# Moving eight subtractions to GpSimd and four weight combinations ahead of the scalings in an MLP up pass

## The chip, the core and the metric

The kernel runs on one core of a Trainium2 chip. Each core has TensorE (PE, matrix products), VectorE (DVE), ScalarE (ACT), GpSimd (POOL) and SyncE (SP, which here issues the transfers). The metric is the device time of one execution in microseconds. Before the change it is 2866.62 us, the median of three runs (2863.16 to 2868.66).

## The reference

The program is a two-layer backbone over 1024 latent tokens and 256 context tokens with model width 1024. Each layer runs token mixers under one input projection, an output projection, and then a squared-ReLU MLP of inner width 4096:

```python
def sq_relu_mlp(h, w1, w2):
    return jnp.square(jax.nn.relu(h @ w1)) @ w2

x = x + g1 * (y @ w_out[l])
h = rmsnorm(x, norm2_g[l]) * (1.0 + sc2) + sh2
x = x + g2 * sq_relu_mlp(h, w_mlp1[l], w_mlp2[l])
```

The context tokens go through the same steps in layer 0 only. The change is in the product `h @ w1` for the latent tokens, the up pass, and in the preparation of its operands.

## The kernel before

**Float32 products from rounded parts.** TensorE multiplies a rounded format. Each operand `a` is therefore split in two: a high part `hi`, which ScalarE makes by a cast, and a low part `lo = a - hi`, a subtraction on VectorE. One product of two split operands takes three matmuls (hi·hi, hi·lo, lo·hi; function `mm3`, lines 94 to 96). The helper `parts` (L1097 to L1100) makes one split: the cast is L1098, the subtraction L1099. In the profile both appear under these lines for nearly every operand of the kernel, so one goes by the names of the tiles.

**Seven products instead of eight.** The up pass multiplies a 2 x 2 arrangement of blocks by a scheme in the manner of Strassen and Winograd. The input `h` (transposed, width by tokens) is cut into width halves and token halves: `11` and `21` (first 512 tokens, group 1) and the second 512 tokens, group 2, which yield `22`. Out of these come the combined operands `T1`, `T2`, `T3`, `T4`. Every operand is four tiles of 128 x 512. On the weights' side, a block `j` of 256 output columns gives two chunks `r[0]`, `r[1]` (128 x 1024 each) and from them two combined chunks: `sa` (L1185, L1186) and `sb` (L1191, L1192). Product numbers and operands: 1 with `11`, 2 with `21`, 5 with `T1`, 7 with `T3`, 6 with `T2`, 3 with `22`, 4 with `T4`. Each product is 4 x 3 = 12 matmuls of 128 x 512.

**The stage around the change.** When the output projection has finished group 1, its tokens are normalized, scaled and split, so operands `11` and `21` are ready early. Group 2 comes last. Meanwhile `prep(j, 0)` splits the first weight chunk of blocks 0 to 3 (the "lead"), and TensorE works at `lead()`: products 1 and 2 of these four blocks. During that time `combine` (L1110 to L1154) scales group 2 (`scaled`: L1106 on VectorE, L1107 on ScalarE), forms the combinations, and splits them: first T1 (L1135), then T3 (L1140), then T2 (L1144) together with the high part of `22` (the cast L1147) and the difference for T4 (L1145); then the four low parts of `22` (L1150); and at the end T4's splits. The low parts of T2, T3 and T4 lie in a shared set of tiles named `x`, those of T1 and `22` in tiles named `al`. In between come `prep(0, 1)` (load both chunks of block 0, form `sa`, split it), `prep(0, 2)` (form `sb`, split it) and `prep(0, 3)` (split the second chunk).

**After it.** `rest` goes through the products 5, 7, 6, 3, 4 of each block. Product 7 is written to a fresh PSUM bank, VectorE adds that bank onto a tile (`v`, L1263), and product 4 is later accumulated into the same bank, so it may begin only when L1263 has read it. L1268 does the same for product 6, without a later use of its bank. For later blocks, `prep(j + 1, i)` runs between the products.

**What sets the order.** Apart from the opening stage, the order on each engine is laid out by the framework's planner before the run: it takes instructions by program order and by when its own cost model thinks them ready. On the chip each engine, and SP's queue of transfers, then works its list strictly in that order and waits at an instruction whose input isn't there. The weight chunks go through two buffers `wraw`; a load waits until the previous user of its buffer has been read.

**GpSimd before.** It runs some subtractions of the same kind in `load_y` (L1058), a few products and memsets, and nothing in the stage of this change.

Of the kernel before, what the change touches and what calls it, by code (L numbers as in the profile page):

```python
# [11 lines left out]
F32 = mybir.dt.float32  # L12
# [25 lines left out]
def fview(a):  # L38
    return a.bitcast(F32)
# [8 lines left out]
class Kern:  # L48
# [1045 lines left out]

    def parts(self, src, hi, lo):  # L1097
        ins = self.nc.scalar.copy(hi, src)  # L1098
        self.nc.vector.tensor_sub(lo, src, fview(hi))  # L1099
        return ins  # L1100

    def scaled(self, x, r, gi, A, sh, f):
# [7 lines left out]
    def combine(self, x, A, sh, hi, lo, tp_, xp, out):  # L1110


        nc = self.nc
        h1 = [xf(x, 1, k) for k in range(KT)]
        h2 = [xf(x, 2, k) for k in range(KT)]
        H = KT // 2
        th = {n: [tp_.tile([128, 512], F32R, name=f"th{n}", bufs=H) for _ in range(H)] for n in (2, 3, 4)}
        tl = {n: [] for n in th}

        def low(n):  # L1120

            tl[n].append(xp.tile([128, 512], F32R, name="x", bufs=XB))
            return tl[n][-1][:]

        def halves(gi):
            return [[a[gi] for a in z[i:i + H]] for i in (0, H) for z in (hi, lo)]

        b11h, b11l, b21h, b21l = halves(1)
        t1h, t1l, b22h, b22l = halves(2)
        out.update({"11": (b11h, b11l), "21": (b21h, b21l), "T1": (t1h, t1l), "22": (b22h, b22l)})  # L1130
        out.update({f"T{n}": (th[n], tl[n]) for n in th})
        r = yield
        for k in range(H):
            self.scaled(x, r, 2, A, sh, k)
            nc.vector.tensor_sub(h1[k], h2[k], h1[k])  # L1135
            self.parts(h1[k], t1h[k][:], t1l[k][:])
            yield
        for k in range(H):
            self.scaled(x, r, 2, A, sh, k + H)
            nc.vector.tensor_sub(h2[k], h2[k + H], h2[k])  # L1140
            self.parts(h2[k], th[3][k][:], low(3))
            yield
        for k in range(H):
            nc.vector.tensor_sub(h1[k], h2[k + H], h1[k])  # L1144
            nc.vector.tensor_sub(h1[k + H], h1[k + H], h1[k])  # L1145
            self.parts(h1[k], th[2][k][:], low(2))
            nc.scalar.copy(b22h[k][:], h2[k + H])  # L1147
            yield
        for k in range(H):
            nc.vector.tensor_sub(b22l[k][:], h2[k + H], fview(b22h[k][:]))  # L1150
        yield
        for k in range(H):
            self.parts(h1[k + H], th[4][k][:], low(4))
            yield  # L1154

    def up(self, l, ctx, B, hi, lo, hp_, hid, filler, last):


        nc, d = self.nc, self.d
        NP, LEAD = DFF // 256, 4  # L1160
        W, E = {}, {}

        def chunk(j, m):
            raw = self.wp.tile([128, 1024], F32, name="wraw", bufs=WRAW)
            nc.sync.dma_start(raw[:], d["w1"][l, 2 * j + m])
            return raw

        def split(src, o=0):
            h, g = (self.wp.tile([128, 1024], F32R, name=n, bufs=WB) for n in ("whi", "wlo"))
            self.parts(src[:, o:], h[:, o:], g[:, o:])  # L1170
            return h, g

        def prep(j, i):

            if i == 0:
                W[j] = [chunk(j, 0)], {}
                W[j][1][0] = split(W[j][0][0])
                return
            r, t = W[j]
            if i == 1:  # L1180
                if j < LEAD:
                    r[:] = [chunk(j, 0)]
                r.append(chunk(j, 1))
                s = hp_.tile([128, 1024], F32, name="sa")
                nc.vector.tensor_add(s[:, :512], r[1][:, :512], r[1][:, 512:])  # L1185
                nc.vector.tensor_sub(s[:, 512:], s[:, :512], r[0][:, :512])  # L1186
                E[j, "sa"] = s
                t[1] = split(s)
            elif i == 2:
                s = hp_.tile([128, 1024], F32, name="sb")  # L1190
                nc.vector.tensor_sub(s[:, :512], r[0][:, :512], r[1][:, :512])  # L1191
                nc.vector.tensor_sub(s[:, 512:], r[0][:, 512:], E[j, "sa"][:, 512:])  # L1192
                t[2] = split(s)
            else:
                t[3] = split(r[1], 0 if ctx else 512)

# [515 lines left out]
    def run(self):  # L1712
        nc, d = self.nc, self.d
        PS = bass.MemoryType.PSUM
        with self.open(name="pad", side="right") as pad, self.open(name="const") as self.cp, self.open(name="w") as self.wp, \
# [13 lines left out]
            hi, lo = self.alloc_act()  # L1729
            with self.open(name="x0") as xp, self.open(name="sp0") as self.sp, self.open(name="ada0") as ap0, self.tc.manual_schedule():  # L1730
                W, accs, Wv = self.opening(xp, ap0, xsrc, hi, lo)
            self.ntmp = 3
            for l in range(DEPTH):
                need_ctx = l < DEPTH - 1
                groups = (0, 1, 2) if need_ctx else (1, 2)
                yh, yl, W, xt = self.mixers(l, xsrc, hi, lo, need_ctx, W, accs, Wv if l == 0 else [])
# [3 lines left out]
                hi, lo = self.alloc_act()  # L1740
# [15 lines left out]
                with self.open(name=f"x{l + 1}", side="right") as xp, self.open(name=f"up{l}") as hp_, contextlib.ExitStack() as right:  # L1756

                    x = {1: [None] * KT, 2: [None] * KT}
                    for gi, f0 in ((2, 0), (1, 0), (2, 4), (1, 4)):
                        for f in range(f0, f0 + 4):  # L1760
                            x[gi][f] = xp.tile([128, 512], F32, name="x", bufs=XB)
                    sh, B = mod[:, 24:32, :], {}
                    prep, lead, rest = self.up(l, need_ctx, B, hi, lo, hp_, hid, ada, start)
                    self.ntmp = 2
                    with self.open(name=f"sp{l + 1}") as self.sp:
                        with self.open(name=f"xc{l + 1}", side="right") as xq:
                            if need_ctx:
                                x.update(self.alloc_x(xq, (0,)))
                            run_all(self.outproj(l, x, xsrc, groups[:-1], yh, yl, W, xt))
                            sums = {gi: self.ssq(x, gi) for gi in groups[:-1]}  # L1770
                            out2 = self.outproj(l, x, xsrc, groups[-1:], yh, yl)
                            for _ in range(3):
                                next(out2)
                            for gi, q in sums.items():
                                keep(x, gi)
                                r = self.rstd(*q)
                                if gi == 0:
                                    self.modulate(x, r, gi, A[1], sh, hi, lo)
                                    next(out2)
                                    continue  # L1780
                                for f in range(KT):
                                    self.parts(self.scaled(x, r, gi, A[1], sh, f), hi[f][gi][:], lo[f][gi][:])
                        self.wide = 1
                        acc = self.sp.tile([128, 512], F32, name="ssq", bufs=2)
                        done = 4 if need_ctx else 3
                        for f in range(done):
                            self.ssq_step(acc, x, 2, f, 0, 512)
                        for f in range(done, KT):
                            next(out2)
                            self.ssq_step(acc, x, 2, f, 0, 512)  # L1790
                            if f >= 4:
                                prep(f - 4, 0)
                        self.wide = 0
                        tp_ = right.enter_context(self.open(name=f"tt{l}", side="right"))
                        blocks = self.combine(x, A[1], sh, hi, lo, tp_, xp, B)
                        next(blocks)
                        next(lead)
                        r = self.rstd(acc, 512)
                        keep(x, 2)
                        next(lead)  # L1800
                        blocks.send(r)
                        for _ in range(3):
                            next(lead)
                            next(blocks)
                        prep(0, 1)
                        next(lead)
                        next(blocks)
                        next(blocks)
                        prep(0, 2)
                        next(lead)  # L1810
                        next(blocks)
                        next(blocks)
                        next(lead)
                        next(blocks)
                        prep(0, 3)
                        run_all(blocks)
                    with self.open(name=f"us{l}") as up_:
                        rest(up_)
                with self.open(name=f"xd{l}") as xp, self.open(name=f"sd{l}") as self.sp, self.open(name=f"we{l}") as wx:
# [35 lines left out]
                    hi, lo = nact  # L1855
# [3 lines left out]
def run_all(g):  # L1859
    for _ in g:  # L1860
        pass
# [148 lines left out]
```

## Time and profile before

| | us |
|---|---|
| Median of the runs | 2866.62 |
| Profiled execution | 2864.0 |
| its span | 2862.2 |
| TensorE busy | 2812.3 |
| VectorE busy | 2206.3 |
| ScalarE busy | 1267.9 |
| GpSimd busy | 105.4 |

The span runs from the first to the last instruction of the profiled execution; the execution's own time is 1.8 us longer. A busy share is an average over stages with different limits, so a stage is judged by its own waits. Matmuls are pipelined: a matmul's row may show 0.39 us while the next one starts 0.23 us behind it. A row of a timeline gives the start, the duration, the engine, the line, the operation, the tiles and, in square brackets, the idle time ahead of it and what ended it. A row of waits reads: who waited, for whom, microseconds in total, times, longest.

### The profile page before, as it was taken

What the parts mean: (1) busy time and instruction counts of PE and PEld (TensorE: products, weight loads), DVE (VectorE), ACT (ScalarE), POOL (GpSimd) and SP (SyncE); (2) the same over time, 40 slices, a digit from 0 to 9 for tenths busy, and PEclk for the clock granted to TensorE, in tenths of its full rate; (3) what the DMA queues carried; (4) which work ended last, traced back from release to release, by engine and by line L of the source; (5) the groups of instructions that cost most, each with busy time, mean ns of one, the idle gap of its engine ahead of it and who ended that gap; (6) DMA issues with size and microseconds to landing.
All of it is one profiled execution on the core that took longest, in us unless ns stands there. A gap on an engine that the chain in (4) does not pass through costs nothing. (4 is left out here: it accounts for less than half of the span.)

```text
span 2862.2 us, 45475 instructions
## 1 busy us (share of the span) xinstructions
PE 2812.3 (98%) x16500; PEld 2376.9 (83%) x16500; DVE 2206.3 (77%) x4917; ACT 1267.9 (44%) x2472; POOL 105.4 (4%) x183
## 2 busy tenths in 40 slices
PE   7999999999999999999999999999999999999998
PEld 4877788889888888888889988888887788888888
DVE  6779988776798777589878768878776887759774
ACT  5333335564553333344545333336555533334443
POOL 1110000010000000000000101000010000000000
PEclk9999999999999999999999999999999999999999
DMA  7433433246446555798977222223346354479672
GB/s 257 145 107 126 144 97 104 91 121 203 152 158 234 189 197 199 262 324 290 327 257 263 72 76 88 71 72 120 119 134 205 129 184 154 145 264 312 211 249 99
DMA packets 279264, 497.40 MB, mean 174 GB/s; under 512 B 23648, under 2 KB 119904, under 8 KB 279040
## 3 DMA queue, kind: packets, MB, share of 16 engines
q1 hardware_dynamic: 279040, 494.50, 51.8%
q8 instruction: 130, 2.13, 0.3%
q14 instruction: 94, 0.77, 0.1%
HBM read 398.82 MB, written 95.59 MB: 173 GB/s over the span
## 5 line engine op out<-in xcount | busy, mean ns | idle before, releaser
L94 PE MATMUL q<-ah,whi 128*128 128x512 f32 (+1 forms) x1472 | 549.9, 374 | 3.3 <-ACT ah L1098 2.7
L96 PE MATMUL q<-ah,wlo 128*128 128x512 f32 (+1 forms) x1472 | 547.4, 372 | 0.8 <-DVE wlo L1099 0.7
L95 PE MATMUL q<-al,whi 128*128 128x512 f32 (+1 forms) x1472 | 548.1, 372 | 0.0
L94 PE MATMUL mm<-ah,whi 128*128 128x512 f32 (+1 forms) x1120 | 387.6, 346 | 2.3 <-ACT whi L88 2.1
L96 PE MATMUL mm<-ah,wlo 128*128 128x512 f32 (+1 forms) x1120 | 385.4, 344 | 0.5 <-DVE wlo L89 0.5
L95 PE MATMUL mm<-al,whi 128*128 128x512 f32 (+1 forms) x1120 | 385.3, 344 | 0.0
L94 PEld LDWEIGHTS q<-ah,whi 128*128 128x128 f32 x1472 | 277.8, 189 | 53.2 <-ACT ah L1098 3.4
L96 PEld LDWEIGHTS q<-ah,wlo 128*128 128x128 f32 x1472 | 277.5, 189 | 50.4 <-DVE wlo L1099 1.7
L95 PEld LDWEIGHTS q<-al,whi 128*128 128x128 f32 x1472 | 277.7, 189 | 48.8 <-issue 1.4
L94 PE MATMUL mm<-whi,ah 128*128 128x512 f32 (+2 forms) x864 | 314.6, 364 | 0.4 <-DVE st L320 0.4
L95 PE MATMUL mm<-wlo,ah 128*128 128x512 f32 (+2 forms) x864 | 307.7, 356 | 0.6 <-DVE wlo L89 0.4
L96 PE MATMUL mm<-whi,al 128*128 128x512 f32 (+2 forms) x864 | 307.5, 356 | 0.0
L94 PEld LDWEIGHTS mm<-ah,whi 128*128 128x128 f32 x1120 | 212.5, 190 | 30.4 <-ACT whi L88 2.5
L96 PEld LDWEIGHTS mm<-ah,wlo 128*128 128x128 f32 x1120 | 212.4, 190 | 26.0 <-DVE wlo L89 1.0
L95 PEld LDWEIGHTS mm<-al,whi 128*128 128x128 f32 x1120 | 212.4, 190 | 25.1 <-issue 0.2
L1098 ACT CAST ah<-raw 128x512 fp32r<-128x512 f32 (+1 forms) x264 | 142.8, 566 | 120.4 <-PE q L96 53.5
L94 PEld LDWEIGHTS mm<-whi,ah 128*128 128x128 f32 x864 | 163.7, 189 | 27.7 <-issue 2.5
L96 PEld LDWEIGHTS mm<-whi,al 128*128 128x128 f32 x864 | 163.7, 189 | 23.2
L95 PEld LDWEIGHTS mm<-wlo,ah 128*128 128x128 f32 x864 | 163.9, 190 | 22.0 <-DVE wlo L89 1.4
L1099 DVE TENSOR_TENSOR al<-raw,ah 128x512 fp32r<-128x512 f32 (+1 forms) x264 | 157.6, 621 | 22.6 <-ACT ah L1098 22.3
L1099 DVE TENSOR_TENSOR wlo<-raw,whi 128x1024 fp32r<-128x1024 f32 x84 | 102.5, 1222 | 74.4 <-ACT whi L1098 71.7
L94 PE MATMUL q<-th,whi 128*128 128x512 f32 x384 | 150.4, 392 | 2.1 <-DVE s L1263 2.0
(306 smaller groups left out, 5232.9 us busy)
## 6 DMA issues: line engine op xcount, KB each, us to landing
raw<-w SPq DMA_DIRECT2D x168, 512.0 KB
raw<-hid SPq DMA_DIRECT2D x104, 512.0 KB
wada<-w_adaT SPq DMA_DIRECT2D x96, 512.0 KB
wraw<-w SPq DMA_DIRECT2D x80, 512.0 KB
hid<-hb SPq DMA_DIRECT2D x128, 256.0 KB
hid<-ht SPq DMA_DIRECT2D x96, 256.0 KB
w<-gscr SPq DMA_DIRECT2D x36, 512.0 KB
wada<-w_ada SPq DMA_DIRECT2D x32, 512.0 KB
```

Of the source, the lines that this page charges most:

```text
L94: mm(out, lh, rh, start=start, stop=False, skip_group_check=True)
L95: mm(out, lh, rl, start=False, stop=False, skip_group_check=True)
L96: mm(out, ll, rh, start=False, stop=stop, skip_group_check=True)
L1098: ins = self.nc.scalar.copy(hi, src)
L1099: self.nc.vector.tensor_sub(lo, src, fview(hi))
```

## The change

`parts` takes an engine for its subtraction. In `combine`, the four low parts of `22` and the four of T4 are made on GpSimd instead of VectorE; those of `22` are now made directly behind their casts, and the loop of its own that they had is gone. In `up`, the four operations that form `sa` and `sb` become functions `mix` and `less`; a new step `prep(0, 4)` calls both for block 0 ahead of `combine`, and with them the loads of block 0's two chunks. `prep(0, 1)` and `prep(0, 2)` then only split. For the other blocks the steps stay as they were.

```diff
-    def parts(self, src, hi, lo):
+    def parts(self, src, hi, lo, eng=None):
         ins = self.nc.scalar.copy(hi, src)
-        self.nc.vector.tensor_sub(lo, src, fview(hi))
+        (eng or self.nc.vector).tensor_sub(lo, src, fview(hi))
         return ins
...
             self.parts(h1[k], th[2][k][:], low(2))
-            nc.scalar.copy(b22h[k][:], h2[k + H])
+            self.parts(h2[k + H], b22h[k][:], b22l[k][:], nc.gpsimd)
             yield
-        for k in range(H):
-            nc.vector.tensor_sub(b22l[k][:], h2[k + H], fview(b22h[k][:]))
         yield
         for k in range(H):
-            self.parts(h1[k + H], th[4][k][:], low(4))
+            self.parts(h1[k + H], th[4][k][:], low(4), nc.gpsimd)
             yield
...
+        def mix(j):
+
+            r = W[j][0]
+            if j < LEAD:
+                r[:] = [chunk(j, 0)]
+            r.append(chunk(j, 1))
+            s = E[j, "sa"] = hp_.tile([128, 1024], F32, name="sa")
+            nc.vector.tensor_add(s[:, :512], r[1][:, :512], r[1][:, 512:])
+            nc.vector.tensor_sub(s[:, 512:], s[:, :512], r[0][:, :512])
+
+        def less(j):
+
+            r = W[j][0]
+            s = E[j, "sb"] = hp_.tile([128, 1024], F32, name="sb")
+            nc.vector.tensor_sub(s[:, :512], r[0][:, :512], r[1][:, :512])
+            nc.vector.tensor_sub(s[:, 512:], r[0][:, 512:], E[j, "sa"][:, 512:])
+            return s
...
+            if i == 4:
+                mix(j)
+                less(j)
+                return
...
             if i == 1:
...
+                if (j, "sa") not in E:
+                    mix(j)
+                t[1] = split(E[j, "sa"])
             elif i == 2:
...
+                t[2] = split(E[j, "sb"] if (j, "sb") in E else less(j))
...
                             if f >= 4:
                                 prep(f - 4, 0)
+                        prep(0, 4)
                         self.wide = 0
                         tp_ = right.enter_context(self.open(name=f"tt{l}", side="right"))
                         blocks = self.combine(x, A[1], sh, hi, lo, tp_, xp, B)
```

More of the change, by code (lines that the diff above doesn't have):

```diff
@@ L1180, in prep @@
             if i == 1:
[L1181 to L1188, printed above, removed]
+                if (j, "sa") not in E:
+                    mix(j)
+                t[1] = split(E[j, "sa"])
             elif i == 2:
[L1190 to L1193, printed above, removed]
+                t[2] = split(E[j, "sb"] if (j, "sb") in E else less(j))
             else:
```

## The prediction

> **What bounds the kernel now.** I read the page first, then the PE waits of the two stretches that the change touches, then VectorE's order inside them. TensorE is busy almost throughout, so only a place where it waits can pay.
>
> ```profile
> span 2862.2 us, 45475 instructions
> PE 2812.3 (98%) x16500; PEld 2376.9 (83%) x16500; DVE 2206.3 (77%) x4917; ACT 1267.9 (44%) x2472; POOL 105.4 (4%) x183
> ```
>
> The combining stage runs at about 790 to 824 us in layer 0 and 2233 to 2265 us in layer 1. The table by stage shows VectorE (the third busy column) full in both; TensorE pays only in the second.
>
> ```profile
> core 0: us, PE busy (x) PEld busy (x) DVE busy (x) ACT busy (x) POOL busy (x), PEclk, DMA share, GB/s
> 790.00:826.00 36.00, 36.00 (x205) 31.73 (x204) 35.59 (x56) 26.74 (x51) 0.00 (x0) 1.00 0.23 81
> 2234.00:2266.00 32.00, 28.76 (x121) 21.98 (x120) 32.00 (x52) 23.91 (x43) 0.00 (x0) 1.00 0.22 74
> ```
>
> TensorE's waits, asked for 785 to 900 us (first row), 2252 to 2266 us (next two) and 2266 to 2345 us (last two):
>
> ```profile
> PE mm L276 <- DVE ssq L245: 0.5, 1, 0.5
> ...
> PE q L94 <- DVE s L1263: 2.0, 1, 2.0
> PE q L95 <- DVE x L1099: 1.1, 3, 0.7
> ...
> PE q L94 <- ACT whi L1098: 0.6, 1, 0.6
> PE q L96 <- DVE wlo L1099: 0.5, 1, 0.5
> ```
>
> Layer 0 loses nothing to the combining; its one wait (L276) comes ahead of it. Layer 1 waits for the low parts of T2 (L1099, read as x), then for L1263, which empties the bank of product 7 before product 4 may add to it and which VectorE reaches only behind all low parts; then twice for weights. In time order, on VectorE, TensorE and TensorE's clock:
>
> ```profile
> 2259.63 0.69 DVE L1099 TENSOR_TENSOR x<-x,th 128x512 fp32r<-128x512 f32 x1
> 2260.37 0.49 PE L95 MATMUL q<-x,whi 128*128 128x512 f32 x1 [0.24 <-DVE x L1099]
> 2262.64 2.50 DVE L1099 TENSOR_TENSOR x<-x,th 128x512 fp32r<-128x512 f32 x4
> 2263.39 0.39 PE L96 MATMUL q<-ah,wlo 128*128 128x512 f32 x1
> 2265.05 0.69 DVE L1263 TENSOR_TENSOR s<-q,s 128x512 f32<-128x512 f32 x1
> 2265.79 0.50 PE L94 MATMUL q<-th,whi 128*128 128x512 f32 x1 [2.02 <-DVE s L1263]
> 2266.88:2270.29 3.41, 3.41 (x10) 2.69 (x9) 3.41 (x6) 2.18 (x3) 0.00 (x0) 0.52 0.02 5
> 2270.24 0.40 PE L94 MATMUL q<-ah,whi 128*128 128x512 f32 x1
> 2283.68 0.39 PE L96 MATMUL q<-th,wlo 128*128 128x512 f32 x1
> ...
> 2286.47 0.39 PE L95 MATMUL q<-al,whi 128*128 128x512 f32 x1
> ```
>
> Four subtractions (L1099 x4) go from 2262.64 to 2265.05: 2.41/4 = 0.60 us each back to back. In layer 0 the same two points are far apart:
>
> ```profile
> 818.40 0.69 DVE L1099 TENSOR_TENSOR x<-x,th 128x512 fp32r<-128x512 f32 x1
> ...
> 823.22 0.69 DVE L1263 TENSOR_TENSOR s<-q,s 128x512 f32<-128x512 f32 x1
> 826.72 0.39 PE L94 MATMUL q<-th,whi 128*128 128x512 f32 x1
> ...
> 827.40 0.39 PE L94 MATMUL q<-th,whi 128*128 128x512 f32 x1
> ```
>
> Three matmuls take 0.68 us, so one is 0.227 us. Product 4 starts at 826.72 without waiting, while L1263 was over at 823.91: **2.8 us of slack** in layer 0. Product 6 starts 24 matmuls before it, at 821.28, and needs its last T2 low after 0.23 + 3 x 0.68 us, at 823.55; it was there at 819.09, 4.5 us early.
>
> **What could be won at most.** In layer 1: the gap from 2263.39 to 2265.79 less one matmul, 2.17 us; half of the 3.41 us at clock 0.52 that follows it, 1.7 us; and the weight waits, five matmuls in 2.79 us instead of 1.13, 1.66 us. Together **5.5 us**. The T2 waits can't be won: the eight subtractions that leave VectorE stood behind the last T2 low (the L1150s and T4's L1099s fill 2260.23 to 2265.05), so nothing ahead of it gets shorter.
>
> **Part 1: eight subtractions per layer from VectorE to GpSimd.** VectorE saves 8 x 0.60 = 4.8 us per layer. GpSimd already does this very operation elsewhere:
>
> ```profile
> L1058 POOL TENSOR_TENSOR al<-wraw,ah 128x512 fp32r<-128x512 f32 x7 | 9.3, 1328 | 23.4 <-ACT ah L1057 15.7 <-PE q L1025 7.7
> ```
>
> 1.33 us each, 10.6 us for eight; GpSimd is otherwise idle here. What speaks against it is what VectorE does meanwhile. Three collisions, and one of another kind:
>
> ```profile
> 2106.14 1.44 POOL L1058 TENSOR_TENSOR al<-yraw,ah 128x512 fp32r<-128x512 f32 x1
> 2107.04 1.62 DVE L89 TENSOR_TENSOR wlo<-wraw,whi 128x1024 fp32r<-128x1024 f32 x1 [0.60 <-ACT whi L88]
> ...
> 2834.06 1.62 POOL L1551 TENSOR_TENSOR x<-x,ssq 128x256 f32<-128x256 f32 x2 [726.48 <-ACT ssq L280]
> 2834.01 3.13 DVE L1553 SCALAR_TENSOR_TENSOR x<-x,consts,ssq 128x256 f32<-128x256 f32 x5 [1.07 <-ACT ssq L280]
> ...
> 19.45 1.96 POOL L82 TENSOR_TENSOR wraw<-wraw 128x378 f32<-128x378 f32 x2 [19.01 <-DMA wraw<-w_kvg]
> 18.69 4.00 DVE L1648 TENSOR_TENSOR x<-x,ssq 128x256 f32<-128x256 f32 x8
> ...
> 132.96 2.57 POOL L82 TENSOR_TENSOR wraw<-wraw 128x252 f32<-128x252 f32 x1 [15.38 <-DMA wraw<-w_j]
> 134.97 0.28 DVE L495 COPY kt<-mm 128x128 f32<-128x128 f32 x1
> ...
> L89 DVE TENSOR_TENSOR wlo<-wraw,whi 128x1024 fp32r<-128x1024 f32 x76 | 93.6, 1233 | 42.0 <-ACT whi L88 40.6
> L82 POOL TENSOR_TENSOR wraw<-wraw 128x378 f32<-128x378 f32 x4 | 3.8, 938 | 176.6 <-DMA raw<-hid 153.5 <-DMA wraw<-w_kvg 23.1
> ```
>
> The L89 that met GpSimd's subtraction took 1.62 us against a mean of 1.23, and ended as if it had begun when GpSimd stopped. A VectorE operation on 256 columns should take about half of 0.60, say 0.33 us at this overhead (an estimate): five would be 1.7 us, but took 3.13, so two GpSimd operations (0.81 each) cost 0.7 each; eight would be 2.7, but took 4.00, so two cost 0.65 each of at most 0.94. VectorE operations with two SBUF inputs thus wait for a GpSimd operation, losing 0.7 to 0.9 of its time: **0.9 to 1.2 us per subtraction, I take 1.1**; the bounds are nothing (no collision) and the full 1.33. In the fourth row GpSimd lost instead: 2.57 us behind a run of VectorE operations, ending just after L495, which reads PSUM. Both happen; large operations look like the first three.
>
> The Trainium skill ("SBUF — State Buffer", section "Who interferes with whom") says that a VectorE instruction with two SBUF inputs and a GpSimd one reading SBUF exclude each other for the whole instruction, the first to issue winning. The trace agrees for L89 and not for the 2.57 us wait, which outlasted several VectorE operations. By the rule the six collisions counted below would cost 6 x 1.33 = 8.0 us where the rows give 6.6, and layer 1 would lose 1.4 us more.
>
> How many of the eight fall ahead of L1263? The "22" ones are released by the casts at L1147, and in layer 1 three of these four begin only here:
>
> ```profile
> 2253.64 1.15 ACT L1147 CAST ah<-x 128x512 fp32r<-128x512 f32 x2
> ```
>
> So from about 2254.3 on GpSimd has work, inside VectorE's unbroken run; T4's subtractions follow. With one VectorE operation between two on GpSimd, a pair takes 1.3 + 0.6 = 1.9 us, so the seven from 2254.3 on last until 2267.6. I count **six ahead of L1263** (four "22", two T4), two behind.
>
> **Part 2: two weight combinations first.** The four operations L1185, L1186, L1191, L1192 keep their count and two DMA loads their buffers; both `wraw` slots were loaded at the same moment already, as they came free. SP's order changes by these two loads moving ahead of `keep`'s stores; the stores before L1106 issue earlier than the second load in both layers.
>
> ```profile
> 790.41 0.69 DVE L1185 TENSOR_TENSOR sa<-wraw 128x512 f32<-128x512 f32 x1 [4.01 <-DMA wraw<-w]
> 2232.78 2.08 DVE L1106 SCALAR_TENSOR_TENSOR x<-x,A,ssq 128x512 f32<-128x512 f32 x3 [2.60 <-ACT ssq L280]
> ...
> 2229.61 0.33 SPq L1165 DMA_DIRECT2D wraw<-w  x1
> DMA  0000000699981000099517699999670000000000
> ```
>
> Layer 0 (first row): VectorE waits for that load until 790.41, already ahead of the scalings; the other three operations, 1.8 us, now also go there, and are missing later: 0 at L1263. Layer 1: issued at 2229.61, its transfer is over near 2232.5 (the DMA strip covers 2228 to 2234, 0.15 us a slice); the scalings begin at 2232.78. So 0.3 us of idle time gets used and the scalings start 4 x 0.60 - 0.3 = 2.1 us later. That delays T1's parts, for which TensorE shows no wait; T3's and T2's came behind these four operations before and gain the 0.3. I take **-0.3 us**; if the planner still puts a scaling first, 0.
>
> **The sum.** Layer 1, L1263: -0.3 - 4.8 + 6 x 1.1 = +1.5 us. Layer 1, T2: its last low is behind four collisions and only the 0.3 is saved, so 2259.63 - 0.3 + 4.4 = 2263.7; the wait there grows, product 4 begins 2263.62 - 2260.37 = 3.25 us after that matmul, and 2263.7 + 0.74 + 3.25 = 2267.7 against 2265.79: +1.9. The later of the two decides: **+1.9**. The half clock and the weight waits I leave as they are, since VectorE stays late. Layer 0: L1263 moves by -4.8 + 6.6 = +1.8, inside 2.8; T2 by 4.4, inside 4.5: **0**. The profiled execution took 2864.0 us (1.8 beyond its span), 2.6 below the median 2866.62 of the runs shown; 2866.6 + 1.9 = **2868.5 us**, +0.07%. A measurement of this kernel can tell about 0.2%, 5.7 us, from no change; this is no change.
>
> **The rivals.**
> - *GpSimd holds up VectorE fully* (slower). All eight collide ahead of L1263 at 1.33: layer 1 -0.3 - 4.8 + 10.6 = +5.5; layer 0 +5.8, of which 2.8 is slack: +3.0, and a gap of that size brings another half-clock spell, 1.7 us. Sum +10.2: 2876.8 us. For it: the first three collisions. Against: two T4 lows probably come after the chain. It decides once layer 0's L1263 is more than 2.8 us late. The Trainium skill ("TensorE: Matmul & The Clock Gate", "What's actually happening") has the clock halve after an idle window of about 3.4 us, and then the 1.7 would not come, 2875.1; but in layer 1 a gap of 2.4 us was followed by it.
> - *No holding up* (faster): L1263 comes at 2259.95, TensorE runs on from product 3 to 4, all 5.5 us are won: 2861 us. For it: VectorE's operations on PSUM don't collide. Against: the chain here is nearly all SBUF with SBUF.
> - *GpSimd starves* as at 132.96: VectorE's chain ends at 2259.95 and then eight at 1.33 run to 2270.6; product 4's last two matmuls take 0.45 more, and the next product begins at 2271.1 where it began at 2270.24: +0.8, and up to +5 if VectorE's next operations slip between; layer 0 0 to +4. About 2869 us.
> - *The planner changes little* or orders something else: 2866.6 us.
>
> **How the numbers follow.** Forecast 0.40, fully held up 0.27, starved 0.16, nothing won 0.11, little change 0.06. Slower by over 0.2% (above 2872.4): the held-up case and a share of the starved, 0.30. Faster (below 2860.9): the free case lies on that edge, 0.09. Within: 0.61. The range reaches from the free case to near the held-up one: 2861 to 2876; the forecast's own, by 0.9 to 1.2 us per collision and the runs' spread, is 2865 to 2872.
>
> **What would show it.** Eight GpSimd subtractions near 1.3 us in each stage; VectorE operations beside them lasting 1.5 us or more instead of 0.69; the wait at L95 for T2's lows above 1.1 us in layer 1 and L1263 near 2266 to 2267; no new wait in layer 0. VectorE's operations at 0.69 us beside GpSimd's, and L1263 near 2260, would prove the forecast wrong towards faster; a wait for L1263 in layer 0 towards slower.

## The result, and the profile after

The changed kernel takes 2876.39 us, median of six runs (2873.12 to 2880.93); the kernel before took 2863.86 in the six runs beside them (2863.16 to 2868.66). The ratio is 1.0035, with a 95% interval of 1.0024 to 1.0046: slower by about 10 us, on the side and near the sum of the rival that GpSimd holds VectorE up fully, and 0.4 us beyond the predicted range, which ended at 2876. The forecast itself was 2868.5 us, no change. The profiled execution took 2877.67 us. The head of its page:

```profile
span 2875.9 us, 45494 instructions
PE 2817.7 (98%) x16500; PEld 2378.4 (83%) x16500; DVE 2211.5 (77%) x4901; ACT 1269.5 (44%) x2472; POOL 145.3 (5%) x199
```

VectorE has 16 instructions less than before and is busy 5.2 us longer; GpSimd has 16 more and is busy 39.9 us longer, 2.5 us for each where 1.33 was counted on.

**Which stage lost.** Both traces hold 16,500 matmuls, so the k-th start of one can be set against the k-th of the other. How much the difference grows across a stretch is what the stretch lost. From 780 to 900 us of the time before (layer 0's up pass) it grows by 8.1 us, from 2225 to 2340 (layer 1's) by 2.1. Elsewhere it drifts by some us from one execution to the next, in every kernel, so only these two figures are used; all runs have them in the table further down.

TensorE's waits in the two stretches (785 to 850, then 2225 to 2300 us); layer 0's first line and layer 1's first line are new, and the former is the sign that the prediction had named for an outcome on the slow side:

```profile
PE q L94 <- DVE s L1275: 3.5, 1, 3.5
PE q L95 <- DVE x L1099: 1.1, 2, 0.7
...
PE q L95 <- POOL x L1099: 2.0, 2, 1.2
PE q L95 <- DVE x L1099: 1.9, 2, 1.0
```

L1275 is the line that was L1263, VectorE's read of product 7's bank. Layer 1 no longer waits for it at all; layer 0, which never did, now waits 3.5 us.

**Layer 0 in order of time**, on VectorE, GpSimd and TensorE; "x2" covers two operations, in brackets stand the idle time before a row and what ended it:

```profile
811.10 1.28 DVE L1145 TENSOR_TENSOR x<-x 128x512 f32<-128x512 f32 x2
813.58 2.39 DVE L1099 TENSOR_TENSOR x<-x,th 128x512 fp32r<-128x512 f32 x2 [1.20 <-POOL al L1099]
815.90 2.32 DVE L1099 TENSOR_TENSOR wlo<-wraw,whi 128x1024 fp32r<-128x1024 f32 x1
818.14 1.78 DVE L1099 TENSOR_TENSOR x<-x,th 128x512 fp32r<-128x512 f32 x1
819.84 2.38 DVE L1144 TENSOR_TENSOR x<-x 128x512 f32<-128x512 f32 x2
822.14 1.28 DVE L1145 TENSOR_TENSOR x<-x 128x512 f32<-128x512 f32 x2
823.35 2.38 DVE L1099 TENSOR_TENSOR x<-x,th 128x512 fp32r<-128x512 f32 x2
825.65 1.77 DVE L1178 TENSOR_TENSOR sa<-wraw 128x512 f32<-128x512 f32 x1
827.35 1.78 DVE L1185 TENSOR_TENSOR sb<-wraw 128x512 f32<-128x512 f32 x1
829.04 0.68 DVE L1179 TENSOR_TENSOR sa<-sa,wraw 128x512 f32<-128x512 f32 x1
829.76 0.69 DVE L1186 TENSOR_TENSOR sb<-wraw,sa 128x512 f32<-128x512 f32 x1
830.84 1.23 DVE L1099 TENSOR_TENSOR wlo<-sa,whi 128x1024 fp32r<-128x1024 f32 x1 [0.39 <-ACT whi L1098]
831.98 0.68 DVE L1275 TENSOR_TENSOR s<-q,s 128x512 f32<-128x512 f32 x1
...
806.42 7.13 POOL L1099 TENSOR_TENSOR al<-x,ah 128x512 fp32r<-128x512 f32 x1 [150.71 <-DVE x L1140]
813.90 5.46 POOL L1099 TENSOR_TENSOR al<-x,ah 128x512 fp32r<-128x512 f32 x3 [0.35 <-ACT ah L1098]
820.05 1.62 POOL L1099 TENSOR_TENSOR x<-x,th 128x512 fp32r<-128x512 f32 x1 [0.69 <-issue]
823.80 4.77 POOL L1099 TENSOR_TENSOR x<-x,th 128x512 fp32r<-128x512 f32 x3 [2.13 <-ACT th L1098]
...
828.86 0.39 PE L96 MATMUL q<-ah,wlo 128*128 128x512 f32 x1
832.72 0.50 PE L94 MATMUL q<-th,whi 128*128 128x512 f32 x1 [3.47 <-DVE s L1275]
```

Before the change, block 1's operations came behind the read at 823.22; the first and the last of the five that now stand ahead of it:

```profile
823.82 0.69 DVE L1185 TENSOR_TENSOR sa<-wraw 128x512 f32<-128x512 f32 x1
...
827.42 1.22 DVE L1099 TENSOR_TENSOR wlo<-sa,whi 128x1024 fp32r<-128x1024 f32 x1
```

This execution entered the stage 0.6 us later than the one before did, so the read at 831.98 instead of 823.22 is 8.1 us late by the stage's own clock. It is made of three things:

- *Seven collisions.* Beside GpSimd's last seven subtractions VectorE's rows are 1.1 us too long: 1.78 instead of 0.69 for one operation, 2.39 instead of 1.28 for two, 2.32 instead of 1.22 for the large split. Seven by 1.1 is 7.7 us.
- *One reused tile.* GpSimd's first subtraction took 7.13 us beside VectorE's unbroken run. The low part that VectorE wants to write at 812.4 goes into a tile that this subtraction still reads, so VectorE stood still for 1.20 us; before, the reader was VectorE itself. (The row names GpSimd as what ended the wait. A low part's two inputs come from VectorE and ScalarE, so only its output tile can have been held by GpSimd.)
- *Five operations put ahead.* L1178, L1185, L1179, L1186 and the low part of `sa` belong to block 1. The planner, which moves VectorE's work up to where its model sees room, now has them ahead of the read. At 0.69 and 1.22 us (0.60 and 1.13 back to back) they are 3.5 us, with the 0.39 us of waiting 3.9.

With the 4.8 us that VectorE was freed of, -4.8 + 3.9 + 7.7 + 1.2 = +8.0, against +8.1. TensorE loses 1.4 us on T2's low parts, 3.6 at the read, and 2.1 more at the same reads of blocks 1 to 3 (0.8, 0.2 and 1.0); the last 1.0 comes in steps of about 0.1 us behind these gaps. That those later reads are late because VectorE is still behind from this stage is likely but not shown: in e9, the same kernel, none of them is late, and in e3, where VectorE is ahead, TensorE loses 0.5 us at block 3's as well.

**Layer 1.** Here the stage began 10.9 us later than before. VectorE, GpSimd, TensorE:

```profile
2255.99 2.45 DVE L1106 SCALAR_TENSOR_TENSOR x<-x,A,ssq 128x512 f32<-128x512 f32 x2
...
2272.86 1.75 DVE L1099 TENSOR_TENSOR x<-x,th 128x512 fp32r<-128x512 f32 x1 [1.18 <-POOL al L1099]
2274.53 0.68 DVE L1275 TENSOR_TENSOR s<-q,s 128x512 f32<-128x512 f32 x1
...
2256.28 1.61 POOL L1099 TENSOR_TENSOR al<-x,ah 128x512 fp32r<-128x512 f32 x1 [137.29 <-ACT ah L1098]
2266.67 9.08 POOL L1099 TENSOR_TENSOR al<-x,ah 128x512 fp32r<-128x512 f32 x3 [8.78 <-ACT ah L1098]
2275.71 7.34 POOL L1099 TENSOR_TENSOR x<-x,th 128x512 fp32r<-128x512 f32 x4
...
2274.66 0.67 PE L95 MATMUL q<-x,whi 128*128 128x512 f32 x1 [1.05 <-DVE x L1099]
2278.11 0.46 PE L94 MATMUL q<-th,whi 128*128 128x512 f32 x1
2280.90 0.50 PE L95 MATMUL q<-x,whi 128*128 128x512 f32 x1 [0.74 <-POOL x L1099]
2283.10 0.50 PE L95 MATMUL q<-x,whi 128*128 128x512 f32 x1 [1.24 <-POOL x L1099]
```

The read at 2274.53 is 1.4 us earlier than before (2263.6 against 2265.05). Ahead of it stand two collisions and one wait: L1106 beside GpSimd's first "22" subtraction (2.45 us for two, where 1.42 is usual), T2's last low part (1.75 us), and 1.18 us for the reused tile. -4.8 + 2 x 1.1 + 1.2 = -1.4. TensorE's loss has moved to both sides of the read: ahead, T2's last low part waits 1.18 us for the reused tile and then 1.1 for GpSimd; behind, T4's low parts are late, because GpSimd's three "22" ones took 9.08 us and the four of T4 7.34, where seven alone would be 9.3.

### The profile page after: what moved, and what is told of

Same layout as the page of the kernel before. It is cut to its first block, busy times and chain, and to the rows that moved or that the text cites. A ratio compares the mean times of both kernels' runs of the same rounds, so it can differ in the third digit from the quotient of the medians.

```text
span 2875.9 us, 45494 instructions
## 1 busy us (share of the span) xinstructions
PE 2817.7 (98%) x16500; PEld 2378.4 (83%) x16500; DVE 2211.5 (77%) x4901; ACT 1269.5 (44%) x2472; POOL 145.3 (5%) x199
## 4 chain that ended last, share of the span: by engine, by line
PE 75%; DVE 10%; issue 6%; DMA 5%; ACT 2%; SPq 1%; POOL 1%; DVEq 0%; ACTq 0%; POOLq 0%
PE q L94 13%; PE q L95 12%; PE q L96 12%; PE mm L94 10%; PE mm L95 9%; PE mm L96 9%; PE q L1048 2%; DMA raw<-hid 1%; DVE wlo L89 1%; DMA wada<-w_adaT 1%; PE q L996 1%; PE q L1014 1%; PE q L725 1%; PE q L986 1%; DVE wada L209 1%
```

## The experiments

All are timed against the kernel before on the same chip. "L0" and "L1" are what the two stretches lost in the profiled execution, in us, by the matmuls' starts as above; every row is set against the one profiled execution of the kernel before.

| run | what differs | ratio to before (95%) | L0 | L1 |
|---|---|---|---|---|
| the change | | 1.0035 (1.0024 to 1.0046) | +8.1 | +2.1 |
| e9 | the change again | 1.0041 (1.0028 to 1.0055) | +7.1 | +1.2 |
| e1 | GpSimd's subtractions alone | 1.0023 (1.0014 to 1.0032) | +3.6 | +2.2 |
| e2 | the two combinations ahead alone | 0.9998 (0.9989 to 1.0007) | 0.0 | +0.3 |
| e3 | GpSimd writes zeros instead | 0.9985 (0.9976 to 0.9994) | +0.6 | -5.6 |
| e10 | GpSimd copies instead | 0.9994 (0.9985 to 1.0004) | +0.8 | -2.8 |
| e11 | all on VectorE, order of the change | 0.9994 (0.9985 to 1.0002) | 0.0 | +0.1 |
| e4 | block 1's operations behind the read | 1.0024 (1.0015 to 1.0033) | +4.9 | +2.5 |
| e5 | only "22" on GpSimd | 1.0019 (1.0010 to 1.0029) | +4.1 | +2.3 |
| e6 | only T4 on GpSimd | 1.0014 (1.0004 to 1.0024) | +3.2 | +1.3 |
| e7 | kernel before, T4's parts behind product 7 | 0.9999 (0.9988 to 1.0011) | +0.1 | +0.3 |
| e8 | e7 with e2 | 1.0006 (0.9997 to 1.0015) | +0.1 | +0.2 |
| e12 | e2, combinations earlier still | 1.0014 (1.0005 to 1.0023) | +1.8 | +3.0 |

The sums of the two columns and the timed ratios (0.1% is 2.9 us) tell the same story in every row, to within some 3.5 us; one interval spans about 3 us to either side.

### Each half alone (e1, e2)

```diff
                                 prep(f - 4, 0)
-                        prep(0, 4)
                         self.wide = 0
```

> Only the GpSimd part of the change; the two weight combinations stay where they were. Theory 'port' (GpSimd's subtractions and VectorE's operations with two SBUF inputs exclude each other, some 1.1 us of VectorE's time per collision): as slow as the whole change, +10 to +13 us on before, with VectorE operations of 1.7 to 1.8 us beside the GpSimd ones in both layers. Rival 'early combinations' (the four operations ahead of the scalings cost the time): near before, within 3 us.

```diff
-            self.parts(h2[k + H], b22h[k][:], b22l[k][:], nc.gpsimd)
+            nc.scalar.copy(b22h[k][:], h2[k + H])
             yield
+        for k in range(H):
+            nc.vector.tensor_sub(b22l[k][:], h2[k + H], fview(b22h[k][:]))
         yield
         for k in range(H):
-            self.parts(h1[k + H], th[4][k][:], low(4), nc.gpsimd)
+            self.parts(h1[k + H], th[4][k][:], low(4))
```

> Only the two weight combinations ahead of the scalings; all subtractions on VectorE as before. Theory 'port': no change, within 2 us of before, and the bank of product 7 is read within 1 us of where it was read before (823.2 and 2265 us). Rival 'early combinations': +8 us or more.

The combinations alone change nothing; the whole loss needs GpSimd's subtractions. Moved alone, they cost 6.6 us by the timed ratio and not the expected 10 to 13. In e1 VectorE pays for only four of them ahead of its read (two at L1106, which takes 3.50 us for two operations at 806.26, and two at block 1's operations); the last six mostly wait instead. GpSimd, then TensorE's largest wait in each stretch:

```profile
816.98 9.96 POOL L1099 TENSOR_TENSOR al<-x,ah 128x512 fp32r<-128x512 f32 x2 [7.77 <-DVE x L1099]
826.89 7.41 POOL L1099 TENSOR_TENSOR x<-x,th 128x512 fp32r<-128x512 f32 x4
...
PE q L95 <- POOL x L1099: 2.2, 3, 1.2
...
PE q L95 <- POOL x L1099: 2.4, 4, 0.7
```

Two subtractions in 9.96 us, then T4's four, for which TensorE waits. Here VectorE's read of product 7 (at 827.94, in a stage that began 1.9 us later) is 2.8 us late, at the edge of its slack. Which of the two engines is held up thus depends on the order around them; TensorE pays either way.

### What in GpSimd's work does it (e3, e10, e11)

```diff
-        (eng or self.nc.vector).tensor_sub(lo, src, fview(hi))
+        if eng:
+            eng.memset(fview(lo), 0.0)
+        else:
+            self.nc.vector.tensor_sub(lo, src, fview(hi))
```

> As the changed kernel, but GpSimd fills the eight low parts with zero instead of subtracting, so that it reads no SBUF: the low parts of operands 22 and T4 are left out of the result. VectorE keeps its shorter list and its new order. Theory 'port': no VectorE operation beside them is lengthened (0.69 us), the 3.5 us wait of layer 0 is gone, and the time is 0 to 6 us below before, since VectorE has 4.8 us less to do per layer. Rival 'order' (in layer 0 five operations of block 1's weights now stand ahead of the read of product 7's bank, 3.5 us of work): the wait in layer 0 stays by 2 us or more and the time above before.

```diff
-        (eng or self.nc.vector).tensor_sub(lo, src, fview(hi))
+        if eng:
+            eng.tensor_copy(lo, src)
+        else:
+            self.nc.vector.tensor_sub(lo, src, fview(hi))
```

> GpSimd copies the operand into the low part's tile instead of subtracting, so the low parts of 22 and T4 hold the operand itself (the result is no longer the reference's); the order on all engines stays that of the changed kernel. GpSimd reads one tile instead of two. If any reading of SBUF by GpSimd shuts VectorE's two-input operations out: VectorE's operations beside the copies take longer by about one copy's own duration (somewhere between the memset's 0.53 and the subtraction's 1.33 us), the read in layer 0 comes 3 to 5 us later than with the memset, and the total lies between the memset's (about 3 us below the kernel before) and the change's (about 10 above), say +2 to +7. Rival, only two-input operations of GpSimd collide: VectorE's operations stay at 0.69 us and the time is that of the memset, -2 to -5 us against before.

```diff
-            self.parts(h2[k + H], b22h[k][:], b22l[k][:], nc.gpsimd)
+            self.parts(h2[k + H], b22h[k][:], b22l[k][:])
...
-            self.parts(h1[k + H], th[4][k][:], low(4), nc.gpsimd)
+            self.parts(h1[k + H], th[4][k][:], low(4))
```

> The changed kernel with all eight subtractions back on VectorE, at the places where the change puts them; the two weight combinations stay ahead of the scalings. It shows what the change's program order alone does. If the five block-1 operations ahead of the read cost 3.5 us by themselves, layer 0's read comes about 3.5 us later than before, 0.7 us more than its slack: layer 0 loses 0 to 1 us, layer 1 0 to 1, total +0 to +2. If order by itself does as much as the collisions, the total is near the change's, +8 to +10.

In e3 VectorE's operations run at 0.69 us beside GpSimd's zeros, with the same five block-1 operations ahead of the read (L1278 here):

```profile
817.01 2.10 POOL L1100 MEMSET x<- 128x512 f32 x4 [33.48 <-ACT ah L1098]
...
816.82 1.29 DVE L1147 TENSOR_TENSOR x<-x 128x512 f32<-128x512 f32 x2
...
824.63 0.68 DVE L1278 TENSOR_TENSOR s<-q,s 128x512 f32<-128x512 f32 x1
```

In e10 the copies collide as well, at a lower price:

```profile
814.44 12.07 POOL L1100 CAST al<-x 128x512 fp32r<-128x512 f32 x1 [3.92 <-ACT x L1110]
826.46 3.74 POOL L1100 CAST x<-x 128x512 fp32r<-128x512 f32 x4
...
2270.19 1.09 DVE L1102 TENSOR_TENSOR x<-x,th 128x512 fp32r<-128x512 f32 x1
...
828.53 0.68 DVE L1278 TENSOR_TENSOR s<-q,s 128x512 f32<-128x512 f32 x1
```

Against the start of their stage (2.2 us later in e3, 4.7 in e10) the three reads in layer 0 come 0.8 us early with zeros, 0.6 late with copies and 8.1 late with subtractions, at one and the same order on VectorE. From zeros to subtractions that is 8.9 us: the seven collisions and the 1.2 us. A copy lengthens VectorE's 0.69 to 1.09, by 0.4 us; its four last ones in 3.74 us are 0.94 each. Both answers of e10's two theories are half right: reading one tile collides, but in layer 0 it took so long to get a turn (12.07 us for one copy) that only 1.4 us of collisions was left ahead of the read; the time stays near e3's.

The Trainium skill ("SBUF — State Buffer", section "Who interferes with whom") says that a VectorE instruction with two SBUF inputs contends with a GpSimd one that reads SBUF and not with one that only writes. Zeros at 0.69 and copies at 1.09 us beside VectorE agree with it.

In e11 the planner leaves block 1's operations behind the read (828.22, in a stage that began 5.15 us later: as before), so it showed that program order costs nothing when VectorE does all the work, and not what the five operations cost. e3 shows that: they use up 3.9 of the 4.8 us that VectorE was freed of.

### The order in layer 0 (e4)

```diff
-                nc.vector.tensor_add(v[:], c[:], v[:])
+                E[j, "va"] = nc.vector.tensor_add(v[:], c[:], v[:])
...
-                        prep(j + 1, i)
+                        with self.tc.issue_after(E[j, "va"].ins) if j == 0 and i < 3 else contextlib.nullcontext():
+                            prep(j + 1, i)
```

> As the changed kernel, but VectorE's operations for block 1's weights are held behind the read of product 7's bank, in layer 0 the order that it had before. Theory 'port' alone: time of the changed kernel within 2 us. Port and order together: in layer 0 the read moves from 832.0 to about 826 us (five operations, 3.5 us, and two collisions less ahead of it), its 3.5 us wait goes, and the time falls by 4 to 6 us against the changed kernel, to some +5 to +8 on before; layer 1 is as in the changed kernel.

TensorE's waits from 836 to 905 us:

```profile
PE q L94 <- DVE s L1275: 2.1, 3, 0.9
```

The read of product 7 is at 831.98 in a stage that began 6.9 us later than before, so it is 1.9 us late, and TensorE does not wait for it in block 0. The collisions didn't go away: T2's low parts still cost 1.6 us, and the row shows the reads of blocks 1 to 3 late instead (why, this run doesn't show; see the remark at layer 0 above). Layer 0 loses 4.9 instead of 8.1 or 7.1. The timed intervals of the change and of e4 overlap, so the gain of 2 to 3 us is read from the traces alone.

### Half of the subtractions (e5, e6)

```diff
-            self.parts(h1[k + H], th[4][k][:], low(4), nc.gpsimd)
+            self.parts(h1[k + H], th[4][k][:], low(4))
```

> As the changed kernel, but only the four low parts of operand 22 on GpSimd; those of T4 back on VectorE. Theory 'port': these four start while VectorE has its longest unbroken run, so all four collide, 4 x 1.1 = 4.4 us against 4 x 0.60 = 2.4 saved: +2 us in layer 1; in layer 0 the same +2 and four operations of block 1's weights (2.4 us) ahead of the read, 4.4 us late against 2.8 us of slack: +1.6 there. About +2 to +6 us on before. Rival 'GpSimd's own 1.3 us is what is late' (VectorE isn't held up): below before, as VectorE has less to do.

```diff
-            self.parts(h2[k + H], b22h[k][:], b22l[k][:], nc.gpsimd)
+            nc.scalar.copy(b22h[k][:], h2[k + H])
             yield
+        for k in range(H):
+            nc.vector.tensor_sub(b22l[k][:], h2[k + H], fview(b22h[k][:]))
```

> As the changed kernel, but only the four low parts of T4 on GpSimd; those of 22 back on VectorE. Theory 'port': these start near the end of VectorE's run and about half collide ahead of the read of product 7's bank: layer 1 -2.4 + 2.2, about 0; layer 0 another 2.4 us of block 1's weights ahead of the read, inside 2.8 us of slack, about 0. Within 3 us of before. Rival 'GpSimd's own 1.3 us is what is late': product 4 waits for its last low part by 2 us or more and the time is +3 us or more.

Four on GpSimd cost 6.4 us ("22") and 4.5 us (T4) in the two stretches, where eight cost 10.2 and 8.3. T4's alone had looked harmless, since they come last; but GpSimd gets through them slowly, and TensorE waits in layer 1. (In layer 0 it loses its 3.2 us mostly at the reads of blocks 2 and 3.)

```profile
2273.73 10.30 POOL L1099 TENSOR_TENSOR x<-x,th 128x512 fp32r<-128x512 f32 x4 [153.14 <-DVE x L1099]
...
PE q L95 <- POOL x L1099: 3.3, 3, 2.0
```

### Without GpSimd: can the order alone win? (e7, e8, e12)

```diff
                 rest(j, 1)
+                run_all(blocks)
                 rest(j, 2)
...
-                        run_all(blocks)
+                        for _ in range(4):
+                            next(blocks)
```

> The kernel before, with nothing on GpSimd, but T4's splits placed in the program behind product 7, so that in layer 1 VectorE reads product 7's bank before T4's four low parts and not behind them. If that read is what ends TensorE's wait in layer 1 (2.0 us, and the half-clock spell of 3.4 us behind it), the read comes at 2262.6 and not 2265.05, the wait all but goes, and the time falls by 3 to 5 us. Rival (T4's low parts are late as well): product 4 then waits for them instead and nothing is won, within 1 us. Layer 0 unchanged in both.

> The same with the two weight combinations ahead of the scalings as in the change (no GpSimd). These cost and gain nothing so far, so the same -3 to -5 us on before; if they help once the read is early, 1 us more.

e8 is the same edit on e2. In e7 the read of product 7 comes ahead of T4's low parts, and its wait in layer 1 is gone. By the matmuls' starts TensorE was 2.3 us ahead of its usual pace there at one point, and gave it all back within 8 us. VectorE, TensorE, and TensorE's clock behind:

```profile
2273.67 0.68 DVE L1186 TENSOR_TENSOR sa<-sa,wraw 128x512 f32<-128x512 f32 x1
...
2275.48 0.50 PE L94 MATMUL q<-ah,whi 128*128 128x512 f32 x1 [1.32 <-ACT whi L1098]
2276.74 0.50 PE L96 MATMUL q<-ah,wlo 128*128 128x512 f32 x1 [0.53 <-DVE wlo L1099]
...
2277.40:2280.60 3.20, 3.20 (x9) 2.46 (x8) 3.17 (x5) 1.56 (x2) 0.00 (x0) 0.51 0.47 108
```

Next to be late is block 1's `sa`, which VectorE forms until 2274.35: its cast and its low part keep TensorE waiting, and half clock follows. e3 had shown that 4.8 us less work on VectorE there is worth 5.6; a new order of the same work is worth nothing.

```diff
+                if j == 0:
+                    r[1] = chunk(0, 1)
                 t[3] = split(r[1], 0 if ctx else 512)
...
+                            if f == 4:
+                                prep(0, 4)
...
-                        prep(0, 4)
```

> All subtractions on VectorE as before; block 0's two weight combinations are formed while VectorE still waits for group 2, behind the fifth square sum, instead of during the scalings. 1.8 to 2.4 us of VectorE's work leave its unbroken run in layer 1. If VectorE's work in that run is what layer 1 waits for: layer 1 is 2 to 3 us shorter, layer 0 unchanged, total -2 to -3 us. If the run's length doesn't matter, or another load or product moves with it: 0 or a little above.

This was to take some 2 us out of that run by forming the combinations in VectorE's idle time before it. It came out 4 us slower than before instead. VectorE, and TensorE's longest wait:

```profile
2235.44 0.69 DVE L1180 TENSOR_TENSOR sa<-wraw 128x512 f32<-128x512 f32 x1 [3.31 <-DMA wraw<-w]
...
PE mm L276 <- DVE ssq L245: 3.5, 1, 3.5
```

VectorE works its list in order. It stood 3.31 us at the weights' load, and behind it in the list were the residual and the square sums that TensorE's L276 needs. With the half clock behind that wait (0.5 from 2248 to 2251 us) TensorE lost 5.2 us; in the run itself it made up 2.2 of them, about what was hoped for. Whether the shorter run gave that, or only TensorE's own lateness, isn't shown. (The edit also loads block 0's second chunk a second time, for its own split.)

### The change again (e9)

No edit.

> The changed kernel unaltered, to see how far the figures of its two stages repeat, and on one chip with the next three. Theory (collisions of GpSimd's subtractions with VectorE's operations, plus a wait for a reused tile, plus five block-1 operations put ahead of the read of product 7's bank): about 10 us above the kernel before, the read in layer 0 some 8 us later than before, VectorE's operations beside GpSimd's at 1.7 to 1.8 us instead of 0.69. Rival (the first profile was an odd one): layer 0 loses 3 to 4 us as with the subtractions moved alone, total 5 to 6 us.

The stages repeat: 8.3 us in both together after 10.2. One thing differs. TensorE's gap at the read is the same (3.84 us between two starts, 3.86 in the first profile), but here half clock follows it. The second row is the first profile's, 3.1 us from nearly the same point of the stage; the figure behind the busy times is the granted clock:

```profile
834.00:837.10 3.10, 3.10 (x9) 2.39 (x8) 3.06 (x5) 2.19 (x3) 0.00 (x0) 0.51 0.20 75
```

```profile
833.50:836.60 3.10, 3.10 (x19) 2.67 (x18) 3.06 (x5) 2.20 (x3) 0.00 (x0) 1.00 0.14 54
```

Nine matmuls instead of nineteen; that cost 1.6 us in e9. No later read of this layer was late there.

## Why the prediction was wrong

**The bound.** Right. That at most 5.5 us could be won, all in layer 1, is what e3 gives: -5.6 there, nothing in layer 0. That the read of product 7 is what decides in layer 1 was too narrow: e7 removed that wait and won nothing. The limit is VectorE's whole run, of which the read is one place.

**The price of a collision.** Right: 1.1 us, in all seven rows of layer 0.

**Layer 0, the step that failed.** "Layer 0: L1263 moves by -4.8 + 6.6 = +1.8, inside 2.8; T2 by 4.4, inside 4.5: 0." The read moved by 8.1 and T2's last low part by 6.0 (it ends at 825.73, 825.1 by the stage's own clock, where 819.09 stood). Three terms were missing. The count of six was made in layer 1 and carried over; in layer 0 all eight cost VectorE something ahead of the read, +8.9 instead of +6.6. The freed time was counted as saved, but the planner filled it with five operations of block 1, +3.9. Of the 8.9 us, 1.2 is a wait that no term had: a tile that VectorE reuses now has a reader on another, slower engine. With the order put right (e4), the read moved by +1.9 and TensorE did not wait for it in block 0, as the sentence has it. Even then its result of 0 falls: T2's margin of 0.1 us didn't hold (1.6 us lost there), and the reads of blocks 1 to 3, which the prediction didn't follow, came late.

**Layer 1.** The sum, +1.9, was met (+2.1, and +1.2 again), but in part by luck, since its parts were others. T2's last low part was forecast 4.1 us late and ended 3.4 late (at 2263.7, that is 2274.6 less 10.9, where 2260.3 stood), by one wait and two collisions instead of four collisions. The read was forecast 1.5 us late and was 1.4 early, since two collisions and one wait stood ahead of it instead of six collisions. The product behind it began 1.4 us late (2267.2), not 1.9. Inside that product T4's low parts, the waits of 0.74 and 1.24 us, cost TensorE 2.3 us, which only the rival that GpSimd starves had. Against that, the half clock, which the prediction left where it was and which had run inside this product, now came ahead of it (granted clock 0.60 from 2274 to 2278 us).

**The combinations.** -0.3 us, or 0 if nothing used the idle time: e2 measured nothing in either layer. What they do together with GpSimd's subtractions (L0 +8.1 and +7.1 against e1's +3.6) was not forecast; how far it is their place in VectorE's list or the planner's other choices that follow from it wasn't tested apart.

**The rivals.** "Fully held up" had the sum, +10.2, and the point from which it decides, layer 0's read more than 2.8 us late. Its parts were others: it gave layer 1 +5.5 and layer 0 +4.7, where 2.1 and 8.1 were measured, and its half clock came in one of two executions. The starving rival was treated as an alternative; it happened beside the collisions, in the same stage: the first subtractions starve, and from the first break in VectorE's run on, the two engines take turns, so VectorE pays for the rest.

## What to carry to other kernels

Moving work off a full engine pays only if the engine that takes it over reads memory in a way that doesn't stop the first; here each 0.60 us moved cost up to 1.1 us on the engine it was taken from, and the last of T4's low parts in layer 1 came 7.0 us late (2272.1 by the stage's own clock, where 2265.1 stood). Count what a planner puts into the freed time, ahead of the operation that matters, before counting that time as saved. A slack measured in one layer must be set against a count made in that layer, and a margin of 0.1 us is none.

## What the hardware showed

- A GpSimd operation of 1.33 us can take 7.13 us beside VectorE (one subtraction at 806.42), and a copy 12.07. VectorE's rows run back to back at 0.60 us meanwhile and lose nothing. GpSimd got in where that row of operations broke: at VectorE's pause at 812.4; in e1's layer 1 at the read of a PSUM bank (L1275 at 2269.30, behind which VectorE's next row takes 1.17 us instead of 0.69); and beside L1106 with no pause at all (2.45 us for two). From there they mostly alternate: 5.46 us for three. The prediction knew both outcomes from single rows, and not that one turns into the other. The section of the Trainium skill named above has whoever issues first hold the ports for one whole instruction; that fits the alternation, and the 7.13 us, which outlast eight VectorE operations begun after it, show that a waiting GpSimd does not get the next turn.
- Half clock is not a matter of the gap's length alone. Gaps of 3.86 and 3.84 us between the same two matmuls were followed by 1.00 in one execution and 0.51 in the other; before, 2.4 us in layer 1 was enough. The Trainium skill ("TensorE: Matmul & The Clock Gate", "What's actually happening") has the clock judged over windows that run freely and do not start anew with the kernel. The different outcomes of two equal gaps agree with that. A price for half clock in a sum is a chance, not a term.
